# Memory projections without their 1/rms, and the rotary angles placed beside the FFN's down projection

## The chip, the core and the metric

The kernel runs on one core of a Trainium2 chip. The metric is the device time of one execution in microseconds (us); the time before is the median of three runs.

## The reference, cut to what matters

Two transformer blocks run one after the other on 256 tokens of 1024 features, all in fp32. The first block has two layers (a gated linear attention with FFN over context and tokens, then a latent attention, MLA, with FFN). The second block has one layer with three mixers; one of these attends to a memory of 256 rows, another uses a partial rotary embedding at given positions:

```python
kvm = rms_norm(mem, mem_norm_g) @ w_mem_kv            # 256 rows, 512 columns
km, vm = jnp.split(kvm, 2, axis=-1)
km = rms_norm(km.reshape(B, N_MEM, MEM_HEADS, HEAD_DIM), mk_norm_g)
...
ang = positions.astype(jnp.float32)[..., None] * inv_freq
cos = jnp.cos(ang)[:, :, None, :]
sin = jnp.sin(ang)[:, :, None, :]
```

The memory and the positions are inputs, so both pieces can be computed at any place ahead of the second block. `rms_norm(mem, g)` is mem * (1/rms of the row) * g. The factor 1/rms belongs to a row of the memory, so it can be applied after the product with the weights as well as before it.

## The kernel before, in words

Activations lie feature-major: 8 tiles of 128 features by 256 tokens. Each fp32 product is made of fp32r matmuls on split operands, hi and lo (`mm3`, lines 336 to 346): three matmuls of 256 columns, or one of 512 and one of 256 where hi and lo of the moving side lie together. Every weight travels the same road in one fixed list (`items`): a transfer by SP's queue into one of three `raw` buffers (line 275), a copy to hi on ScalarE (line 295), a subtraction to lo on VectorE (line 301) into one of four `wp` buffers. `weight()` asks for conversions three units ahead of the one that TensorE reads.

The order on each engine comes from the framework's scheduler. It takes program order as priority but puts an instruction forward when the engine would be free and its inputs are there, by its own estimate of durations. `tc.issue_after(x)` holds an instruction behind x on its engine.

The stages around the change, in program order:

- **MLA attention**, loop over `hd` from 0 to 9 (lines 1583 to 1592). Scores and softmax of head `hd`, transposes of head `hd-1`, values of head `hd-2`; steps 8 and 9 have only the ends of the last heads. In the same loop `mst.add` squares the memory tile by tile (ScalarE) and adds up (VectorE), which gives 1/rms of the memory's rows later. The query parts of head k lie in the half `MAIN` of the buffer `h`, feature tile k.
- **MLA output projection** (lines 1594 to 1600): 8 units of 8x3 matmuls. The first three units run together. After each unit `residual` (line 1146, VectorE) adds to `xT`, and `Stats.add` squares on ScalarE (line 538) and adds on VectorE (line 544, tile `sqa`). Woven into it are the steps of `normed_steps` for the memory: per feature tile a product with gain and 1/rms from PSUM (line 714, VectorE), a copy to hi (line 350, ScalarE) and a subtraction to lo (line 351, VectorE), into `h`'s half `MAIN`.
- **Memory key projection** (lines 1622 to 1624), 2 units of 24 matmuls. After the first 4 feature tiles (12 matmuls) the residual's statistics are closed (`st.rstd`: column sums by matmuls on line 518, a transpose on line 489, a square root on line 494, a reciprocal on line 496), then spread by two TensorE transposes (line 483), and `modulated` (lines 700 to 703) makes the input of the FFN. `m_evac` takes the keys from PSUM (line 1618) and squares them for the head norms.
- **Rotary angles** (lines 1632 to 1659): a small transfer of the positions by GpSimd's queue and 33 elementwise instructions of 128x256 on GpSimd; no other work is asked of GpSimd here.
- **FFN of the second layer**: 44 up units (22 steps of the loop over j, two units each), then a down projection of 8 outputs m with 4 weight units each (two of 6 and two of 5 feature tiles). `side()` is advanced once per j: sine and cosine at the seventh step, held behind a ScalarE instruction by `issue_after`, then the key norms.
- **End of the FFN**: the statistics of the new residual, `normed` for the second block, and the memory's value projection (lines 1691 to 1695).

`Stats` has a switch `ahead`: behind the square of the fourth tile it runs a dummy Sqrt (lines 499 to 505), so that the table for Sqrt is loaded before it is needed.

Of the kernel before, what the change touches and what calls it, by code (L numbers as in the profile page):

```python
# [10 lines left out]
F32 = mybir.dt.float32  # L11
F32R = mybir.dt.float32r
I32 = mybir.dt.int32
# [199 lines left out]
def body(tc, A, where, out, dbg=None):  # L213
# [48 lines left out]
    def width(i):  # L262
        us = items[i][1]
        return 2048 if us is None else sum(k * n for _, k, n in us)
# [6 lines left out]
    def top_up(n=NRAW):  # L271
        while at["dma"] < min(at["free"] + n, len(items)):
            j = at["dma"]
            r = wpool.tile([128, 2048], F32, tag="raw", name="raw", bufs=NRAW)
            SP.dma_start(r[:, :width(j)], items[j][0])
            raws[j] = r
            at["dma"] += 1

# [41 lines left out]
    class Two:  # L320


        def __init__(self, t):
            self.t = t
# [28 lines left out]
    def drain(g):  # L353
        for _ in g:
            pass
# [11 lines left out]
    def weave(main, fill, r=1):  # L367

        for _ in main:
            for _ in range(r):  # L370
                next(fill, None)
# [77 lines left out]
    def C(nm, grp="ca"):  # L449
        o, n = where[grp, nm]  # L450
        return ctile[grp][:, o:o + n]

    def vec(nm, i=0, n=1):
        o, _ = where[nm]
        return vecs[:, o + i:o + i + n]
# [50 lines left out]
    class Stats:  # L506

        def __init__(self, k, n, eng=None, halves=False, ahead=True):  # L510
            self.ahead = ahead and eng is not None
            self.k, self.n, self.c, self.sq, self.eng, self.mm = k, n, 0, None, eng, 0
            self.ns = None if halves else smbank()

# [14 lines left out]
        def add(self, t, square=True):  # L529
            self.flush()  # L530
            self.c += 1
            if not square:
                self.sq = t
                return
            n, inner = self.n, self.eng is not None and self.c < self.k
            head = inner and self.c == 1
            sq = tmp(512, "sqa" if head else "sq", 1 if head else 3)
            act = S.activation(sq[:, :n], t, AF.Square)
            if self.ahead and self.c == 4:
                table(AF.Sqrt, act)  # L540
            if head:
                self.acc = sq
            elif inner:
                self.eng.tensor_add(self.acc[:, :n], self.acc[:, :n], sq[:, :n])
            else:
                self.sq = sq
# [135 lines left out]
    def make_amp(layer, which, gname):  # L682

        need(layer, which * 3)
        need(layer, which * 3 + 1)
        for c in range(2):
            V.scalar_tensor_tensor(amp[:, layer, which, c, :], ada[layer][:, c, which * 24 + 8:which * 24 + 16],
                                   1.0, vec(gname, layer * 8, 8), op0=ALU.add, op1=ALU.mult)
# [19 lines left out]
    def normed_steps(src, gname, s, rr, dst, nb=None, ds=None, pool=()):  # L708
        nb = nb or spread(rr, 256)
        ds = ds or s  # L710
        hh, hl = dst[0], dst[1]
        for k in range(KT):
            u = tmp(512, "u", 2)
            V.scalar_tensor_tensor(u[:, :256], src[:, k, s], vec(gname, k), nb[:, :256], op0=ALU.mult, op1=ALU.mult)
            split_to(hh[:, k, ds], hl[:, k, ds], u[:, :256], G if k in pool else V)
            yield
# [857 lines left out]
    def mla_v(hd, PT):  # L1574
        po = mmbank()
        for kb in range(4):
            T.matmul(po[:, :256], vv[kb][:, hd * 128:(hd + 1) * 128], PT[:, kb, :], start=(kb == 0), stop=(kb == 3))  # L1577
        split_to(oh[0][:, hd, :256], oh[1][:, hd, :256], po[:, :256])

    memt = apool.tile([128, KT, 256], F32, name="memt")  # L1580
    G.dma_start(memt, A["memT"])
    mst = Stats(KT, 256, V, ahead=False)
    for hd in range(10):
        if hd >= 2:
            mst.add(memt[:, hd - 2, :])
        if hd < 8 and hd not in Pq:
            Pq[hd] = mla_s(hd)
        if 0 <= hd - 1 < 8:
            PTq[hd - 1] = mla_t(hd - 1, Pq.pop(hd - 1))
        if 0 <= hd - 2 < 8:  # L1590
            mla_v(hd - 2, PTq.pop(hd - 2))
    make_amp(1, 1, "norm_ffn")
    st = Stats(KT, 256, V)
    f = proj(both(I_mo), oh, HALF, lambda ps, m: residual(ps, m, 1, 2, (1,), st))
    next(f)
    mrr = mst.rstd(1024)
    weave(f, normed_steps(memt, "mem_g", HALF, mrr, h, None, MAIN))
    drain(f)
    mp.close()
    if dbg is not None and "x1a" in dbg:  # L1600
# [11 lines left out]
    kraw = lpool.tile([128, 2, 256], F32, name="kraw")  # L1612
    mhd = []

    def m_evac(ps, m):
        if m == 0:
            mhd.append(Heads(2, 256, 64, True))
        S.activation(kraw[:, m, :], ps, AF.Copy, scale=vec("mkg"))
        mhd[0].add(ps)


    f = proj(both([I_mem[0]]), h, MAIN, m_evac, 0)
# [3 lines left out]
    next(f)  # L1626
    modulated(1, 1, 1, spread(rr, 256), h, HALF)
    drain(f)

    ep_ = ExitStack()  # L1630
    epool = phase["pool"] = ep_.enter_context(tc.tile_pool(name="epool", bufs=1))
    post = tmp(256, "post", 1, I32)
    G.dma_start(post, A["pos"])


    ang = tmp(256, "ang", 1)
    G.tensor_copy(ang, post)
    G.tensor_scalar(ang, ang, C("invf", "cl"), None, op0=ALU.mult)
    twopi = Fraction("6.28318530717958647692528676655900576839433879875021164194988918461563")

    def fpieces(x, bits, n):
# [5 lines left out]
            yield float(v)  # L1647
            r -= v

    MAGIC = 12582912.0  # L1650
    kk, kv_ = tmp(256, "angk", 1), tmp(256, "angv", 1)
    for period, bits, n in ((twopi * 4096, 7, 8), (twopi, 11, 4)):
        G.tensor_scalar(kk, ang, float(1 / period), None, op0=ALU.mult)
        G.tensor_scalar(kk, kk, MAGIC, None, op0=ALU.add)
        G.tensor_scalar(kk, kk, MAGIC, None, op0=ALU.subtract)
        for v in fpieces(period, bits, n):
            G.tensor_scalar(kv_, kk, -v, None, op0=ALU.mult)
            G.tensor_add(ang, ang, kv_)
    G.tensor_scalar(ang, ang, math.pi, -math.pi, op0=ALU.min, op1=ALU.max)
    def side():  # L1660
        for _ in range(6):
            yield
        with tc.issue_after(mark["act"].ins):
            S.activation(sin2, ang, AF.Sin)
            S.activation(kk, ang, AF.Sin, scale=0.5)
        G.tensor_mul(kk, kk, kk)
        G.tensor_scalar(cos2, kk, -2.0, 1.0, op0=ALU.mult, op1=ALU.add)

        yield
        mhd[0].rstd()  # L1670
        yield
        for m in range(2):
            V.tensor_mul(km[:, m, :], kraw[:, m, :], mhd[0].spread(m))
            yield

    st = []

    def resid1(ps, m, last):
        if m == 0:
            st.append(Stats(KT, 256, V))  # L1680
        residual(ps[:, 256:], m, 1, 5, (1,), None)
        residual(ps[:, :256], m, 1, 5, (1,), st[0])

    ffn(1, h, (1,), False, resid1, side(), s=HALF)
    if dbg is not None and "x1b" in dbg:
# [6 lines left out]
    for t in range(2):  # L1692
        ps = mmbank()
        gemm_t(ps[:, :256], ws, h, 2 + t)
        S.activation(vm[:, t, :], ps[:, :256], AF.Copy)
    ep_.close()
    l2 = phase["pool"] = lp.enter_context(tc.tile_pool(name="l2pool", bufs=1))
    lcnt = C("lcnt", "cl").rearrange("p (t k) -> p t k", t=2)
# [261 lines left out]
```

## Time and profile before

| | us |
|---|---|
| runs (three) | 1309.72, 1310.82, 1315.43 |
| median | 1310.82 |
| the profiled execution, its time | 1309.43 |
| its span in the profile | 1307.7 |
| TensorE busy | 1265.2 (97%) |
| VectorE busy | 1076.0 (82%) |
| ScalarE busy | 748.3 (57%) |
| GpSimd busy | 84.8 (6%) |

The profile is one execution; times in it count from the start of its span. A row of a time line gives start, duration, engine, line, operation, output and inputs, and in brackets how long the engine sat idle before it and who released it. Matmuls overlap, so two of them started 0.12 us apart can each show 0.28 us. The engines are PE (TensorE; PEld its weight loads), DVE (VectorE), ACT (ScalarE), POOL (GpSimd) and SPq (SyncE's DMA queue).

### The profile page before, as it was taken

To read this page: it belongs to the slowest core of one execution; us is meant where nothing else is said; L and a number is where in the kernel's file an instruction comes from. 1 tells how busy PE (TensorE), PEld (TensorE's weight loads), DVE (VectorE), ACT (ScalarE), POOL (GpSimd) and SP (SyncE) were. 2 spreads that over 40 slices of the span, in tenths; PEclk is the share of its full clock that TensorE was granted. 3 is DMA by queue.
4 is the path that set the end of the run, shared out by engine and by line. 5 is a ranking of instruction groups with operands and counts; after the bars stand their busy time and mean duration, and the time that the engine had idled before them with its cause. 6 is when DMAs were issued, how large, how long until landed. Compare 5 with 4: busy or idle time off the path is not lost.

```text
span 1307.7 us, 20138 instructions
## 1 busy us (share of the span) xinstructions
PE 1265.2 (97%) x7612; PEld 1082.2 (83%) x7612; DVE 1076.0 (82%) x2261; ACT 748.3 (57%) x1324; POOL 84.8 (6%) x99
## 2 busy tenths in 40 slices
PE   6899999999999999999999998999999899999998
PEld 3779888898888888878987797888889777888887
DVE  3597987779999899879757878999757986899964
ACT  4686354444442244433476755887656777777742
POOL 0000000000000000000002046000000630000000
PEclk9999999999999999999999998999999899999999
DMA  9542344325445654446323113555555321455453
GB/s 375 194 163 95 134 170 148 129 92 188 172 163 195 228 185 179 141 140 217 134 81 129 65 47 130 197 190 184 170 196 180 142 98 65 162 195 200 175 192 109
DMA packets 32497, 207.55 MB, mean 159 GB/s; under 512 B 3760, under 2 KB 5040, under 8 KB 12176
## 3 DMA queue, kind: packets, MB, share of 16 engines
q1 hardware_dynamic: 31968, 204.17, 43.8%
q0 software_dynamic: 432, 2.10, 0.5%
q8 instruction: 60, 0.98, 0.3%
q14 instruction: 37, 0.30, 0.1%
HBM read 205.20 MB, written 1.05 MB: 158 GB/s over the span
## 4 chain that ended last, share of the span: by engine, by line
PE 82%; DVE 9%; ACT 4%; DMA 2%; issue 2%; POOL 1%; SPq 0%; POOLq 0%; DVEq 0%; ACTq 0%
PE mm L345 18%; PE mm L341 16%; PE mm L343 15%; PE mm L342 15%; PE mm L346 9%; DVE wp L301 2%; DMA a<-in_ada_dram 1%; DVE u L654 1%; ACT wp L295 1%; PE mm L1577 1%; DMA raw<-in_w_ada_dram 1%; PE sm L1024 1%; PE mm L1837 1%; PE sm L634 1%; PE mm L1046 1%
## 5 line engine op out<-in xcount | busy, mean ns | idle before, releaser
L301 DVE TENSOR_TENSOR wp<-raw,wp 128x1024 fp32r<-128x1024 f32 (+2 forms) x314 | 350.5, 1118 | 63.8 <-ACT wp L295 63.0
L295 ACT ACTIVATE wp<-raw 128x1024 fp32r<-128x1024 f32 (+2 forms) x316 | 305.0, 970 | 168.5 <-PE mm L343 87.8
L341 PE MATMUL mm<-hp,wp 128*128 128x512 f32 (+1 forms) x1004 | 346.4, 346 | 2.3 <-ACT hp L350 1.7
L342 PE MATMUL mm<-hp,wp 128*128 128x512 f32 (+1 forms) x1004 | 342.5, 342 | 3.1 <-DVE wp L301 3.1
L343 PE MATMUL mm<-hp,wp 128*128 128x512 f32 (+1 forms) x1004 | 338.8, 341 | 0.9 <-DVE hp L703 0.9
L345 PE MATMUL mm<-hp,wp 128*128 128x512 f32 x664 | 231.3, 394 | 0.6 <-DVE hp L351 0.5
L654 DVE SCALAR_TENSOR_TENSOR u<-raw,cb 128x512 f32<-128x512 f32 x320 | 204.8, 686 | 30.3 <-DMA raw<-in_w_ada_dram 25.3
L341 PEld LDWEIGHTS mm<-hp,wp 128*128 128x128 f32 x1004 | 191.6, 191 | 30.2 <-issue 5.7
L342 PEld LDWEIGHTS mm<-hp,wp 128*128 128x128 f32 x1004 | 192.1, 191 | 24.7 <-DVE wp L301 3.5
L343 PEld LDWEIGHTS mm<-hp,wp 128*128 128x128 f32 x1004 | 190.8, 191 | 22.7 <-DVE hp L703 1.6
L346 PE MATMUL mm<-hp,wp 128*128 128x256 f32 x664 | 184.4, 278 | 0.6 <-DVE wp L301 0.6
L345 PEld LDWEIGHTS mm<-hp,wp 128*128 128x128 f32 x664 | 124.4, 187 | 29.8 <-DVE hp L351 0.9
L346 PEld LDWEIGHTS mm<-hp,wp 128*128 128x128 f32 x664 | 125.0, 188 | 1.5 <-DVE wp L301 0.9
L345 PE MATMUL mm<-ap,wp 128*128 128x512 f32 x352 | 122.1, 392 | 0.0
L346 PE MATMUL mm<-ap,wp 128*128 128x256 f32 x352 | 98.4, 279 | 0.0
L1193 ACT ACTIVATE cv<-mm,vecs 128x512 f32<-128x512 f32 (+1 forms) x47 | 35.5, 765 | 78.5 <-PE mm L343 75.4
L345 PEld LDWEIGHTS mm<-ap,wp 128*128 128x128 f32 x352 | 66.0, 188 | 14.6
L343 PE MATMUL mm<-ap,wp 128*128 128x512 f32 (+1 forms) x198 | 72.5, 366 | 0.7 <-DVE ap L351 0.7
L341 PE MATMUL mm<-ap,wp 128*128 128x512 f32 (+1 forms) x198 | 72.7, 367 | 0.4 <-ACT ap L350 0.4
L342 PE MATMUL mm<-ap,wp 128*128 128x512 f32 (+1 forms) x198 | 72.4, 366 | 0.0
L346 PEld LDWEIGHTS mm<-ap,wp 128*128 128x128 f32 x352 | 66.3, 188 | 0.0
L341 PE MATMUL mm<-wp,hp 128*128 128x256 f32 (+1 forms) x192 | 58.4, 304 | 0.1
(327 smaller groups left out, 1893.9 us busy)
## 6 DMA issues: line engine op xcount, KB each, us to landing
raw<-in_up_dram SPq DMA_DIRECT2D x66, 1024.0 KB, 4.8
raw<-in_w_ada_dram SPq DMA_DIRECT2D x40, 1024.0 KB, 4.9
raw<-in_dn_dram SPq DMA_DIRECT2D x48, 704.0 KB, 4.0
raw<-in_gla_in_dram SPq DMA_DIRECT2D x12, 1024.0 KB, 5.6
raw<-in_in_dram SPq DMA_DIRECT2D x9, 1024.0 KB, 4.7
a<-in_ada_dram SPq DMA_DIRECT2D x8, 1024.0 KB, 19.5
raw<-in_gla_out_dram SPq DMA_DIRECT2D x4, 1024.0 KB, 5.8
raw<-in_mla_out_dram SPq DMA_DIRECT2D x4, 1024.0 KB, 4.7
```

Of the source, the lines that this page charges most:

```text
L295: S.activation(hi, r, AF.Copy)
L301: V.tensor_sub(w[:, 1, :kt * c], r, hi)
L341: T.matmul(ps, lhs[0], rhs[0], start=first, stop=False)
L342: T.matmul(ps, lhs[1], rhs[0], start=False, stop=False)
L343: T.matmul(ps, lhs[0], rhs[1], start=False, stop=last)
L345: T.matmul(ps.rearrange("p (a t) -> p a t", a=2), lhs[0], rhs[2], start=first, stop=False)
L346: T.matmul(ps[:, 256:], lhs[1], rhs[0], start=False, stop=last)
L634: T.matmul(nb, lhs, self.hl[j], start=(j == 0), stop=(j == 1))
L654: V.scalar_tensor_tensor(tmp(512, "u", 2), raws[n][:, ks], 1.0, cb[:, c, hf * 512:hf * 512 + 512], op0=ALU.mult, op1=ALU.mult, accum_out=p ...
L1024: T.matmul(pk[:, q * 256:(q + 1) * 256], kt_[:, q * 128:(q + 1) * 128], vv[:, t, q * 256:(q + 1) * 256], start=True, stop=True)
L1046: T.matmul(o, sm[:, q, v * 128:(v + 1) * 128], ep[:, d * 2 + q, blk(t)], start=False, stop=(n == len(use) - 1))
L1193: mark["act"] = S.activation(t[:, :n], ps, AF.Identity, bias=vec(cb, j), scale=vec(cw, 44 + j))
```

## The change

The memory goes into its projections as mem * gain, without 1/rms. The eight hi and lo steps for it (one ScalarE and one VectorE instruction each) move into steps 8 and 9 of the attention loop; the weave with `normed_steps` goes. The factor 1/rms is kept as a tile `mnb` (all partitions, one column per row of the memory) and as a column `mcol` (two TensorE transposes). Keys are multiplied with `mnb` as they leave PSUM, values get `mcol` as the scale of their copy. The angles become a function that `side()` calls at the 21st of 22 steps; the positions now come by SP's queue, behind the newest weight transfer; sine and cosine are taken behind the residual of m = 5 in the down projection, without `issue_after`; `ahead` becomes a number, and the Sqrt table of that stage comes behind the seventh square instead of the fourth.

```diff
@@ top_up
-            SP.dma_start(r[:, :width(j)], items[j][0])
+            mark["raw"] = SP.dma_start(r[:, :width(j)], items[j][0])
@@ Stats.add
-            if self.ahead and self.c == 4:
+            if self.c == self.ahead:
                 table(AF.Sqrt, act)
@@ the attention loop
             mla_v(hd - 2, PTq.pop(hd - 2))
+        if hd >= 8:
+            for k in range(4 * hd - 32, 4 * hd - 28):
+                g = vec("mem_g", k)
+                S.activation(h[0][:, k, MAIN], memt[:, k, :], AF.Copy, scale=g)
+                V.scalar_tensor_tensor(h[1][:, k, MAIN], memt[:, k, :], g, h[0][:, k, MAIN],
+                                       op0=ALU.mult, op1=ALU.subtract)
@@ the MLA output projection
     next(f)
     mrr = mst.rstd(1024)
-    weave(f, normed_steps(memt, "mem_g", HALF, mrr, h, None, MAIN))
     drain(f)
@@ the memory's key projection
+    mnb = lpool.tile([128, 256], F32, name="mnb")
+    S.activation(mnb, spread(mrr, 256)[:, :256], AF.Copy)
+    mcol = lpool.tile([128, 2], F32, name="mcol")
     def m_evac(ps, m):
         if m == 0:
             mhd.append(Heads(2, 256, 64, True))
-        S.activation(kraw[:, m, :], ps, AF.Copy, scale=vec("mkg"))
-        mhd[0].add(ps)
+        u = tmp(512, "u", 2)[:, :256]
+        V.tensor_mul(u, ps, mnb)
+        S.activation(kraw[:, m, :], u, AF.Copy, scale=vec("mkg"))
+        mhd[0].add(u)
...
     drain(f)
+    pt = smbank()
+    for t in range(2):
+        T.transpose(pt[:, t * 128:t * 128 + 128], mnb[:, t * 128:t * 128 + 128], ident)
+    S.activation(mcol, pt[:, 0:256:128], AF.Copy)
@@ the angles: the same GpSimd instructions, now in a function
+    def angles():
+        post = tmp(256, "post", 1, I32)
+        with tc.issue_after(mark["raw"].ins):
+            SP.dma_start(post, A["pos"])
...
+        return ang, kk
     def side():
-        for _ in range(6):
-            yield
-        with tc.issue_after(mark["act"].ins):
-            S.activation(sin2, ang, AF.Sin)
-            S.activation(kk, ang, AF.Sin, scale=0.5)
-        G.tensor_mul(kk, kk, kk)
-        G.tensor_scalar(cos2, kk, -2.0, 1.0, op0=ALU.mult, op1=ALU.add)
-        yield
         mhd[0].rstd()
         yield
         for m in range(2):
             V.tensor_mul(km[:, m, :], kraw[:, m, :], mhd[0].spread(m))
             yield
+        for _ in range(17):
+            yield
+        rot.extend(angles())
+        yield
@@ the FFN's residual
-            st.append(Stats(KT, 256, V))
+            st.append(Stats(KT, 256, V, ahead=7))
         residual(ps[:, 256:], m, 1, 5, (1,), None)
         residual(ps[:, :256], m, 1, 5, (1,), st[0])
+        if m == 5:
+            ang, kk = rot
+            S.activation(sin2, ang, AF.Sin)
+            S.activation(kk, ang, AF.Sin, scale=0.5)
+            G.tensor_mul(kk, kk, kk)
+            G.tensor_scalar(cos2, kk, -2.0, 1.0, op0=ALU.mult, op1=ALU.add)
@@ the memory's value projection
-        S.activation(vm[:, t, :], ps[:, :256], AF.Copy)
+        S.activation(vm[:, t, :], ps[:, :256], AF.Copy, scale=mcol[:, t:t + 1])
```

## Rows read from the trace of the kernel before

**Rows 1.** The page's chain that ended last, shares of the span by engine.
```profile
PE 82%; DVE 9%; ACT 4%; DMA 2%; issue 2%; POOL 1%; SPq 0%; POOLq 0%; DVEq 0%; ACTq 0%
```

**Rows 2.** Windows: start:end, length, busy of PE, PEld, DVE, ACT, POOL, clock, DMA.
```profile
747.00:752.00 5.00, 5.00 (x28) 4.32 (x27) 3.51 (x8) 2.58 (x8) 0.00 (x0) 1.00 0.00 0
...
786.00:791.50 5.50, 5.50 (x48) 5.50 (x47) 5.50 (x10) 3.22 (x7) 5.08 (x5) 1.00 0.42 170
791.50:795.70 4.20, 0.25 (x3) 0.05 (x2) 4.20 (x7) 1.62 (x3) 3.94 (x4) 0.88 0.66 250
...
798.00:801.40 3.40, 3.40 (x21) 3.35 (x16) 0.80 (x3) 1.90 (x4) 3.06 (x5) 0.50 0.85 306
```

**Rows 3.** Time line of PE around the end of the MLA output projection.
```profile
771.33 0.38 PE L483 MATMUL sm<-ca,rr 128*128 128x128 f32 x2
...
791.47 0.28 PE L343 MATMUL mm<-hp,wp 128*128 128x256 f32 x1
795.72 0.44 PE L518 MATMUL sm<-sqa,ones 128*32 128x64 f32 x8 [3.98 <-DVE sqa L544]
...
799.07 0.41 PE L342 MATMUL mm<-hp,wp 128*128 128x256 f32 x1
799.28 0.41 PE L343 MATMUL mm<-hp,wp 128*128 128x256 f32 x1
```

**Rows 4.** PE groups, 766.1 to 791.55: line, operation, tiles, shape, count, busy, mean ns.
```profile
L341 PE MATMUL mm<-hp,wp 128*128 128x256 f32 x68 | 19.5, 287 | 0.0
```

**Rows 5.** DVE groups by form, 771 to 796: busy us, mean ns, idle before.
```profile
L301 DVE TENSOR_TENSOR wp<-raw,wp 128x1024 fp32r<-128x1024 f32 x8 | 10.8, 1345 | 0.0
L351 DVE TENSOR_TENSOR hp<-u,hp 128x256 fp32r<-128x256 f32 x8 | 5.2, 656 | 0.1
L544 DVE TENSOR_TENSOR sqa<-sqa,sq 128x256 f32<-128x256 f32 x6 | 4.4, 727 | 0.0
L714 DVE SCALAR_TENSOR_TENSOR u<-memt,vecs,sm 128x256 f32<-128x256 f32 x8 | 3.7, 476 | 2.0 <-PE sm L483 1.9
```

**Rows 6.** DVE groups by form, 810 to 920 (the FFN's up projection).
```profile
L301 DVE TENSOR_TENSOR wp<-raw,wp 128x1024 fp32r<-128x1024 f32 x40 | 48.7, 1218 | 0.8 <-ACT wp L295 0.4
...
L351 DVE TENSOR_TENSOR ap<-cv,ap 128x256 fp32r<-128x256 f32 x19 | 7.9, 417 | 0.1
```

**Rows 7.** DVE groups by form, 930 to 985 (the FFN's down projection).
```profile
L544 DVE TENSOR_TENSOR sqa<-sqa,sq 128x256 f32<-128x256 f32 x6 | 2.5, 419 | 0.0
```

**Rows 8.** Time line of DVE where the FFN ends and the second block begins.
```profile
990.58 0.48 DVE L1146 SCALAR_TENSOR_TENSOR xT<-mm,ada,xT 128x256 f32<-128x256 f32 x1
...
992.25 0.25 DVE L489 STREAM_TRANSPOSE rs<-sm 128x64 f32<-128x64 f32 x1
...
993.82 0.87 DVE L714 SCALAR_TENSOR_TENSOR u<-xT,vecs,sm 128x256 f32<-128x256 f32 x2 [0.79 <-PE sm L483]
```

**Rows 9.** Windows late in the up projection and inside the down projection.
```profile
912.00:920.00 8.00, 8.00 (x49) 7.06 (x48) 7.84 (x16) 6.23 (x12) 0.00 (x0) 1.00 0.34 115
...
940.00:960.00 20.00, 20.00 (x117) 17.76 (x116) 12.06 (x20) 9.51 (x13) 0.00 (x0) 1.00 0.58 199
```

**Rows 10.** Time line of ACT: first sine, last Silu of the FFN, load for Sqrt.
```profile
849.97 0.40 ACT L1664 ACTIVATE sin<-ang 128x256 f32<-128x256 f32 x1
...
931.55 0.42 ACT L1226 ACTIVATE cv<-cv 128x256 f32<-128x256 f32 x1
...
960.54 1.28 ACT L504 ACT_TABLE_LOAD   x1
```

**Rows 11.** Issue on SP's queue of the third transfer of down-projection weights.
```profile
920.32 0.33 SPq L275 DMA_DIRECT2D raw<-in_dn_dram  x1
```

**Rows 12.** POOL groups by form, 767 to 808: the two largest of the angles.
```profile
L1658 POOL TENSOR_TENSOR ang<-ang,angv 128x256 f32<-128x256 f32 x12 | 13.0, 1086 | 1.0
L1657 POOL TENSOR_SCALAR angv<-angk 128x256 f32<-128x256 f32 x12 | 11.4, 953 | 1.0
```

**Rows 13.** Waits of ACT for POOL, second block: total us, times, longest.
```profile
ACT cvp L1731 <- POOL cacp L1732: 1.7, 4, 0.8
```

More of the change, by code (lines that the diff above doesn't have):

```diff
@@ L506, in body, with __init__ @@
     class Stats:
-        def __init__(self, k, n, eng=None, halves=False, ahead=True):
-            self.ahead = ahead and eng is not None
+        def __init__(self, k, n, eng=None, halves=False, ahead=4):
+            self.ahead = ahead if eng is not None else 0
             self.k, self.n, self.c, self.sq, self.eng, self.mm = k, n, 0, None, eng, 0
@@ L1581, in body @@
     G.dma_start(memt, A["memT"])
-    mst = Stats(KT, 256, V, ahead=False)
+    mst = Stats(KT, 256, V, ahead=0)
     for hd in range(10):
@@ L1628, in body @@
     drain(f)
+    pt = smbank()
+    for t in range(2):
+        T.transpose(pt[:, t * 128:t * 128 + 128], mnb[:, t * 128:t * 128 + 128], ident)
+    S.activation(mcol, pt[:, 0:256:128], AF.Copy)
     ep_ = ExitStack()
     epool = phase["pool"] = ep_.enter_context(tc.tile_pool(name="epool", bufs=1))
[L1632 to L1638, printed above, removed]
     twopi = Fraction("6.28318530717958647692528676655900576839433879875021164194988918461563")
@@ L1648, in fpieces @@
             r -= v
[L1650 to L1659, printed above, removed]
-    def side():
-        for _ in range(6):
-            yield
-        with tc.issue_after(mark["act"].ins):
-            S.activation(sin2, ang, AF.Sin)
-            S.activation(kk, ang, AF.Sin, scale=0.5)
-        G.tensor_mul(kk, kk, kk)
-        G.tensor_scalar(cos2, kk, -2.0, 1.0, op0=ALU.mult, op1=ALU.add)
-        yield
+    def angles():
+        post = tmp(256, "post", 1, I32)
+        with tc.issue_after(mark["raw"].ins):
+            SP.dma_start(post, A["pos"])
+        ang = tmp(256, "ang", 1)
+        G.tensor_copy(ang, post)
+        G.tensor_scalar(ang, ang, C("invf", "cl"), None, op0=ALU.mult)
+        MAGIC = 12582912.0
+        kk, kv_ = tmp(256, "angk", 1), tmp(256, "angv", 1)
+        for period, bits, n in ((twopi * 4096, 7, 8), (twopi, 11, 4)):
+            G.tensor_scalar(kk, ang, float(1 / period), None, op0=ALU.mult)
+            G.tensor_scalar(kk, kk, MAGIC, None, op0=ALU.add)
+            G.tensor_scalar(kk, kk, MAGIC, None, op0=ALU.subtract)
+            for v in fpieces(period, bits, n):
+                G.tensor_scalar(kv_, kk, -v, None, op0=ALU.mult)
+                G.tensor_add(ang, ang, kv_)
+        G.tensor_scalar(ang, ang, math.pi, -math.pi, op0=ALU.min, op1=ALU.max)
+        return ang, kk
+    def side():
         mhd[0].rstd()
@@ L1674, in side @@
             yield
+        for _ in range(17):
+            yield
+        rot.extend(angles())
+        yield
+    rot = []
     st = []
```

## The prediction, made before the change was run

> **What bounds the kernel now.** I read the chain of waits first: TensorE holds 82% of it and VectorE 9% [rows 1]. So a step is worth something only where TensorE waits for it. Next come the windows around the edited lines. In the attention TensorE is busy throughout at full clock, VectorE 3.51 us of 5 and ScalarE 2.58 [rows 2]. Late in the MLA output projection VectorE is busy without a gap, 5.50 of 5.50, with GpSimd beside it at 5.08; then TensorE falls to 0.25 of 4.20 us, and from 798 to 801.4 its granted clock is 0.50 [rows 2]. The reader should see one place: VectorE late, TensorE idle, then TensorE at its lower level, 1.2 instead of 2.4 GHz.
>
> The time line of TensorE names the wait: the last matmul starts at 791.47, and the column sum at 795.72 sat idle 3.98 us for the running sum of squares on VectorE [rows 3]. Afterwards two matmuls start 0.21 us apart [rows 3]. Up to the stop there were 3 x 68 = 204 of them in some 25.4 us, 0.12 us each [rows 4], so TensorE had no gap before it: 192 are the output projection, 12 the first quarter of the memory's keys. The projection itself therefore ends 12 x 0.12 = 1.4 us earlier, at about 790.1.
>
> Why VectorE is late: between 771 and 796 it makes 10.8 us of weight conversions, 5.2 us of lo parts of the memory, 3.7 us of products with gain and 1/rms, and 4.4 us of running sums [rows 5]. Three of these groups are slower than where GpSimd rests: the conversion takes 1345 ns against 1218 [rows 5, 6], the lo part 656 against 417 for the same operation and shape [rows 5, 6], the running sum 727 against 419 [rows 5, 7]. The product that reads PSUM shows no such spread: 476 ns beside GpSimd [rows 5]. So GpSimd's angles cost VectorE 8 x 0.13 + 8 x 0.24 + 6 x 0.31 = 4.8 us in this stretch.
>
> **What the change removes.** VectorE loses from the stretch 3.7 us of products and 5.2 us of lo parts [rows 5], and of the 4.8 us of GpSimd's slowing the 2.9 that fell on what stays. That is 11.8 us of work out of a stretch of 24 in which it had no gap. It fell 795.72 - 791.55 = 4.2 us behind TensorE; with 11.8 us less it is no longer behind, and the running sum is ready before TensorE asks.
>
> So the wait of 3.98 us goes [rows 3]. The stretch at the lower clock behind it goes too, since it follows the only stop of TensorE here: from 795.72 to about 801.4, 5.7 us at 0.21 us a matmul instead of 0.12, of which 5.7 x (1 - 0.12/0.21) = 2.4 us are lost [rows 3, 4]. Together -6.4 us. From 801.4 on TensorE is fed, so nothing more can be gained here.
>
> **What is late next.** The last residual still has to pass square, column sum, transpose, root, spread. The same chain stands at the end of the FFN, where GpSimd rests: residual at 990.58, transpose at 992.25, first product of the next stage at 993.82 [rows 8], 3.2 us, and about 1 us more for its hi and lo. In the new kernel the residual starts near 790.3, so the FFN's first input is there near 794.6. TensorE meanwhile has 48 matmuls of keys, 5.8 us from 790.1, column sums and spread aside: until about 796. The cover is 1.3 us longer than the chain. The key products with `mnb` are two VectorE instructions more, near 0.42 us each by the two-input rows [rows 6]. The first stands ahead of the FFN's modulation and the second inside it; queued behind are the modulated tiles, and TensorE waits for those. The 1.3 us of cover hide both, so 0; without the cover, 0.8.
>
> **What it adds.** (1) Two transposes for `mcol`: a pair shows 0.38 us on TensorE [rows 3], and no other engine hides TensorE's own time. +0.4. (2) Eight ScalarE copies and eight VectorE instructions in the attention. They are independent of the heads still running once head k's scores are done, so the scheduler may put them into any idle gap from there, not only the two last steps. VectorE has 1.5 us free in five, ScalarE 2.4 [rows 2]: the room is there. But a softmax step can queue behind one. Bounds: 0 if they all fall in gaps, and 8 x 0.2 = 1.6 us if each costs a head half of a 0.42 us instruction. A gain is excluded, since TensorE has no gap there. Nearer to the row is the low end, as VectorE is 30% idle: +0.3. (3) Positions by SP's queue: one short transfer behind the newest weights. The weight transfers of the down projection use 0.58 of the DMA engines [rows 9]; it passes between them, 0. If the queue had no room it would hold a weight by less than its own length, hidden by three units of weights ahead. (4) The Sqrt load of 1.28 us [rows 10] moves from the fourth to the seventh square, still beside a down projection in which ScalarE is busy 9.51 of 20 [rows 9]: 0. Sine, cosine, their two GpSimd products and the scale on the values' copy lie there too or replace like by like: 0.
>
> (5) **The angles beside the FFN.** They are asked for at step 21 of 22, behind the third transfer of down-projection weights, which now issues at 920.32 [rows 11] and then about 6 us earlier. Two groups of twelve took 24.4 us beside a full VectorE [rows 12]; the whole chain of 33 at that rate is some 34 us. So its first 6 to 8 us lie beside the end of the up projection, where VectorE is busy 7.84 of 8 [rows 9], and the rest beside the down projection, 12.06 of 20 [rows 9]. By the trace VectorE loses 4.8 in 24, about 0.2 us per us, so 1.2 to 1.6 us there; weights are converted three units of some 2.8 us ahead, which hides it: 0. Bounds 0 and 1.6; a gain is excluded, since TensorE is busy 8.00 of 8 there [rows 9].
>
> The Trainium skill, "SBUF — State Buffer", section on the two sides of SBUF, says that VectorE with two SBUF inputs and GpSimd lock one shared port pair, and that the loser is blocked for the whole instruction. By that rule each VectorE instruction of this kind beside the angles could lose up to one GpSimd instruction, and this change would move the stop rather than remove it. The rows agree in which instructions slow down, and show 0.13 to 0.31 us each, not a whole GpSimd instruction of 0.95 to 1.09.
>
> **The sum.** -6.4 + 0.4 + 0.3 = -5.7 us, against the profiled execution's 1309.4: 1303.7. The median of the runs is 1310.8, 1.4 above that execution, so I forecast 1305.1. About 0.5%, 6.6 us, is what a measurement of this kernel can tell from no change; the border is 1304.3.
>
> **Rivals.**
> *A, the forecast.* Own range 1303 to 1307, 0.66. Runs before scatter by over 1 us to below, and with both additions at nothing the sum is -6.4, so a good part lies past the border: 0.30 of this 0.66.
>
> *B, the stop comes back as a wait for the modulated input.* The keys' inputs are now ready long before their turn. If the scheduler uses their 48 matmuls as filler inside the output projection, TensorE has nothing left when that ends and idles for the chain of 4.3 us, minus little, and again drops to the lower clock: +4 to +6, 1309 to 1311. For it: the scheduler did put 12 of them ahead of the column sum. Against it: up to 791.5 TensorE has no gap to fill [rows 4]. 0.12.
>
> *C, the angles' collision.* If VectorE loses more beside GpSimd than [rows 5 to 7] show, the end of the up projection is where it hurts, since VectorE is 98% busy there [rows 9]. Six to eight GpSimd instructions of about 1 us [rows 12], each holding back a VectorE instruction, make 6 to 8 us, of which the weights ahead hide about 5: +1 to +3, 1306 to 1308. This is the rule of "SBUF — State Buffer" at its full price. 0.10.
>
> *D, slower: the sine stops ScalarE.* Nothing holds the sine behind a given instruction any more. If the scheduler takes GpSimd's chain for shorter than it is, it puts the sine early, as far forward as the last Silu, at 931.55 in the old time line [rows 10], some 925 in the new. ScalarE then waits for the angles until about 917 + 34 = 951, and behind it queue all weight conversions. Three units of down-projection weights ahead carry TensorE some 5.7 us; of 26 us, 20 are left, and 2.4 for the clock: 1305.1 + 22.4 = 1327.5. It decides from a lateness of 5.7 us on, and turns into a slowdown past the border from about 15. Against it: where the second block hands ScalarE's products to GpSimd, ScalarE waited only 1.7 us in four waits [rows 13], so GpSimd's durations are not far misjudged; and at its own place, behind m = 5, the sine is some 15 us later than the angles. 0.12, of which 0.10 past the border.
>
> **How the numbers follow.** Faster: 0.30, from A. Slower: 0.10, from D. The rest is 0.60: what is left of A, B, C and the mild end of D. The range takes in A, B and C, 0.88, with half a us below A for scatter: 1302.5 to 1311.5.
>
> **What would show it.** In the profile after: no wait of the column sum on line 518 over 0.5 us, clock 1.00 through the output projection and the keys, GpSimd idle between 770 and 806, running sums back near 420 ns there, and the FFN's first matmul about 6 us earlier with nothing given back until the second block. B would show as an idle of TensorE in front of the FFN's first matmuls, C as conversions near 1.4 us and a wait of TensorE late in the up projection, D as a wait of ScalarE for GpSimd at the sine. The forecast is wrong if the stop stays although VectorE is free there: then the wait was not VectorE's load but the chain itself.

## The result, and the profile after

The changed kernel takes 1330.47 us (median of 4 runs, 1326.89 to 1333.78), the kernel before 1310.49 us (4 runs, 1309.72 to 1315.43). The ratio is 1.0143, with a 95% interval of 1.0119 to 1.0166: slower by about 19 us. The forecast of 1305.1 us, with a range up to 1311.5, was wrong. It came out as rival D had it, which the prediction put at 1327.5 us and gave 0.12.

In the chain that ended last, by engine, GpSimd has 3% where [rows 1] had 1%, at VectorE's expense:

```profile
PE 83%; DVE 6%; ACT 5%; POOL 3%; DMA 2%; issue 2%; SPq 0%; POOLq 0%; ACTq 0%; DVEq 0%
```

TensorE's waits from 780 on show the place (engine, line, what it waited for; us in total, times, longest):

```profile
PE mm L345 <- ACT wp L295: 15.2, 1, 15.2
PE sm L1851 <- DVE P L1526: 4.6, 3, 2.0
PE sm L634 <- issue: 3.9, 1, 3.9
PE mm L346 <- DVE wp L301: 1.5, 2, 0.9
```

The wait of the column sum in front of the FFN (line 518, [rows 3]) is gone from the list. In its place TensorE waits 15.2 us, once, inside the down projection, for a weight conversion by ScalarE. The time line of ScalarE says why that conversion was late:

```profile
930.44 0.42 ACT L350 ACTIVATE ap<-cv 128x256 fp32r<-128x256 f32 x1 [0.61 <-DVE cv L1227]
931.20 0.85 ACT L295 ACTIVATE wp<-raw 128x768 fp32r<-128x768 f32 x1 [0.34 <-PE mm L346]
952.74 0.42 ACT L1703 ACTIVATE sin<-ang 128x256 f32<-128x256 f32 x1 [20.69 <-POOL ang L1678]
953.06 0.40 ACT L1704 ACTIVATE angk<-ang 128x256 f32<-128x256 f32 x1
953.37 0.72 ACT L295 ACTIVATE wp<-raw 128x640 fp32r<-128x640 f32 x1
```

The sine on line 1703 stands right behind a weight conversion that ended at 932.05. ScalarE takes its instructions in order, so it waited there 20.69 us for the angles, and the next conversion of weights came only at 953.37. The angles were still being made. These are the first, two middle and the last of their 33 instructions in the time line of GpSimd, 921.53 to 952.71:

```profile
921.53 0.69 POOL L1667 CAST ang<-post 128x256 f32<-128x256 int32 x1 [153.52 <-DVE wp L301]
...
947.08 0.85 POOL L1676 TENSOR_SCALAR angv<-angk 128x256 f32<-128x256 f32 x1
948.01 0.72 POOL L1677 TENSOR_TENSOR ang<-ang,angv 128x256 f32<-128x256 f32 x1
...
952.31 0.40 POOL L1678 TENSOR_SCALAR ang<-ang 128x256 f32<-128x256 f32 x1
```

The windows around the stop (start:end, length, busy of PE, PEld, DVE, ACT, POOL, clock) show everything but GpSimd at rest (TensorE's 3.94 us lie ahead of the stop), and TensorE at its lower level, 1.2 GHz, behind the stop:

```profile
935.00:951.00 16.00, 3.94 (x23) 3.16 (x21) 0.00 (x0) 0.00 (x0) 14.47 (x19) 0.74 0.00 1
951.00:957.00 6.00, 2.80 (x7) 2.09 (x8) 2.66 (x4) 3.75 (x7) 3.12 (x5) 0.50 0.17 32
957.00:965.00 8.00, 8.00 (x40) 6.88 (x39) 4.55 (x7) 2.77 (x5) 0.00 (x0) 0.82 0.68 246
```

The place that the prediction was about did what it said. The same stretches as in [rows 2], after the change:

```profile
786.00:791.50 5.50, 5.50 (x52) 5.37 (x54) 3.90 (x7) 3.00 (x5) 0.00 (x0) 1.00 0.56 195
791.50:795.70 4.20, 4.20 (x49) 4.11 (x50) 2.92 (x6) 2.46 (x5) 0.00 (x0) 1.00 0.58 185
798.00:801.40 3.40, 3.40 (x22) 2.48 (x21) 3.22 (x7) 1.43 (x5) 0.00 (x0) 1.00 0.40 118
```

TensorE is busy through all of them at full clock, GpSimd is silent, and VectorE has room. Its operations are quick again where [rows 5] had 1345 and 727 ns (groups by form, 771 to 796):

```profile
L301 DVE TENSOR_TENSOR wp<-raw,wp 128x1024 fp32r<-128x1024 f32 x9 | 10.9, 1220 | 2.2 <-ACT wp L295 2.2
L544 DVE TENSOR_TENSOR sqa<-sqa,sq 128x256 f32<-128x256 f32 x6 | 2.5, 420 | 0.1
```

**Where the 17.4 us between the two spans lie** (1325.1 less 1307.7). A common base is needed, since executions differ already ahead of the edited lines: I take the first matmul of line 1566, at 731.8 before and 731.2 after. From there to the first down matmul it is 196.5 us before and 193.8 after, -2.7. The down projection, first matmul to last, takes 79.7 instead of 60.9, +18.8. From there to the end of the span it is 320.4 instead of 318.5, +1.9. With the -0.6 of the base that is 17.4. So 5.3 us were won in front of the FFN (its first column group ends at 807.16 instead of 813.1, less the base's 0.6), 2.6 of them were given back in the up projection, and the down projection cost 18.8.

### The profile page after: what moved, and what is told of

Read it like the earlier page. It is cut to its first block, busy times and chain, and to the rows that moved or that the text cites. A ratio compares the mean times of both kernels' runs of the same rounds, so it can differ in the third digit from the quotient of the medians.

```text
span 1325.1 us, 20142 instructions
## 1 busy us (share of the span) xinstructions
PE 1269.9 (96%) x7614; PEld 1083.5 (82%) x7614; DVE 1070.1 (81%) x2255; ACT 746.0 (56%) x1324; POOL 77.7 (6%) x98
## 4 chain that ended last, share of the span: by engine, by line
PE 83%; DVE 6%; ACT 5%; POOL 3%; DMA 2%; issue 2%; SPq 0%; POOLq 0%; ACTq 0%; DVEq 0%
PE mm L341 16%; PE mm L345 16%; PE mm L342 16%; PE mm L343 16%; PE mm L346 8%; DVE wp L301 2%; DMA a<-in_ada_dram 1%; ACT wp L295 1%; PE mm L1577 1%; POOL angv L1676 1%; PE sm L1024 1%; PE mm L1046 1%; POOL ang L1677 1%; PE mm L1861 1%; DVE u L654 1%
## 5 line engine op out<-in xcount | busy, mean ns | idle before, releaser
L342 PEld LDWEIGHTS mm<-hp,wp 128*128 128x128 f32 x1004 | 191.9, 191 | 24.6 <-DVE wp L301 3.5
L345 PE MATMUL mm<-ap,wp 128*128 128x512 f32 x352 | 125.1, 399 | 15.2 <-ACT wp L295 15.2
L345 PEld LDWEIGHTS mm<-ap,wp 128*128 128x128 f32 x352 | 67.3, 191 | 31.2 <-ACT wp L295 15.5
## 6 DMA issues: line engine op xcount, KB each, us to landing
a<-in_ada_dram SPq DMA_DIRECT2D x8, 1024.0 KB, 18.8
```

The lines of the kernel that those rows point to most:

```text
L342: T.matmul(ps, lhs[1], rhs[0], start=False, stop=False)
L345: T.matmul(ps.rearrange("p (a t) -> p a t", a=2), lhs[0], rhs[2], start=first, stop=False)
```

## The experiments

The kernels came in three groups, each against runs of the kernel before on the same chip. The table gives, of each profiled execution, the way from the first matmul of line 1566 to the first down matmul ("to down"), the down projection and the rest to the end of the span, in us.

| kernel | ratio to before, 95% | to down | down | rest |
|---|---|---|---|---|
| before | 1 | 196.5 | 60.9 | 318.5 |
| changed | 1.0143 (1.0119 to 1.0166) | 193.8 | 79.7 | 320.4 |
| e1, changed, sine held | 0.9995 (0.998 to 1.0009) | 193.8 | 62.1 | 320.4 |
| e2, memory's part alone | 1.0004 (0.9985 to 1.0022) | 192.5 | 62.1 | 323.8 |
| e3, angles' part alone | 1.0107 (1.0088 to 1.0126) | 191.5 | 78.1 | 323.7 |
| e4, changed, shorter chain | 1.0048 (1.0032 to 1.0065) | 193.8 | 71.3 | 318.9 |
| e5, e12, angles' part, sine held | 0.9953 (0.9937 to 0.9969), 0.9958 (0.9943 to 0.9974) | 191.9, 191.9 | 60.9, 61.5 | 321.8, 318.7 |
| e6, e1 with the key norm put back | 0.9978 (0.9964 to 0.9992) | 192.1 | 62.1 | 321.9 |
| e11, e5 with the key norm put back | 0.9928 (0.991 to 0.9947) | 190.5 | 60.9 | 319.0 |
| e7, before again | one execution, 1313.51 us | 196.5 | 60.9 | 320.5 |
| e8, e1 again | one execution, 1319.08 us | 193.8 | 62.1 | 322.0 |
| e9, e1, held behind block 1 | one execution, 1322.74 us | 195.5 | 71.8 | 322.1 |
| e10, e1, held behind block 2 | one execution, 1311.48 us | 193.9 | 63.4 | 322.2 |

Single profiles scatter too: the rest is 2.0 us longer in e7 than in the first profile of the same kernel, 1.6 in e8 than in e1. And in e3 and e9 "to down" begins with 3.4 us at a granted clock of 0.50 (from 734.5 and 734.2), 1.7 us lost that no other profile has there.

**The sine held back (e1).** In the changed kernel, with the square of the residual remembered at each output block:

```diff
-            S.activation(sin2, ang, AF.Sin)
-            S.activation(kk, ang, AF.Sin, scale=0.5)
+            with tc.issue_after(mark["sq"].ins):
+                S.activation(sin2, ang, AF.Sin)
+                S.activation(kk, ang, AF.Sin, scale=0.5)
```

> The changed kernel, with the sine held behind the square of the residual of m = 5 on ScalarE. Theory Q (queue): the scheduler put the sine where it believed GpSimd's chain to end, some 20 us too early, and the weight conversions queued behind it. Then the wait of ScalarE for GpSimd and the 15.2 us wait of TensorE are gone, the down projection takes 61 us as before instead of 79.7, and what is left is the hand-over won ahead of the FFN: 1305 to 1309. Theory P (port): GpSimd beside the down projection slows the conversions on VectorE by their shared port; then the place of the sine does not matter and the time stays at 1325 to 1331. Theory M (memory part): the new steps of the memory cost more than they save; then it stays over 1313.

Measured: 1310.33 us against 1311.25, a little over the 1305 to 1309 expected. The sine moved behind the square of block 5, where the angles had long been there (time line of ScalarE):

```profile
972.94 0.42 ACT L538 ACTIVATE sq<-xT 128x256 f32<-128x256 f32 x1 [0.32 <-DVE xT L1146]
973.27 0.40 ACT L1704 ACTIVATE sin<-ang 128x256 f32<-128x256 f32 x1
973.57 0.40 ACT L1705 ACTIVATE angk<-ang 128x256 f32<-128x256 f32 x1
```

It waits for nothing, TensorE's 15.2 us are gone, and the down projection takes 62.1 us. Nothing was changed but the place of two instructions in ScalarE's order, so that place is the cause of the loss, some 19 us (1.0143 against 0.9995). GpSimd's angles lie beside the down projection as before, so contention of VectorE and GpSimd is not the cause.

**One part alone (e2, e3).** e2 has the memory's projections without 1/rms, and the angles in their old place; e3 has the angles beside the down projection, and the memory as before; its sine has no hold. Cut to their core, e2 against the changed kernel and e3 against the kernel before:

```diff
     def side():
-        mhd[0].rstd()
...
-        rot.extend(angles())
+        for _ in range(6):
+            yield
+        with tc.issue_after(mark["act"].ins):
+            S.activation(sin2, ang, AF.Sin)
...
```

```diff
-    ang = tmp(256, "ang", 1)
-    G.tensor_copy(ang, post)
...
+    def angles():
+        post = tmp(256, "post", 1, I32)
+        with tc.issue_after(mark["raw"].ins):
+            SP.dma_start(post, A["pos"])
...
+        rot.extend(angles())
```

> Only the memory's part of the change; angles, sine, key norm and positions as before. If VectorE's own work (8.9 us less in the stretch that was 4.2 us late) was the cause of the stop in front of the FFN, the stop of 3.98 us goes though GpSimd still works beside it: 1303 to 1308. If the slowing by GpSimd was the cause, the stop stays for the most part: 1309 to 1312. Theory M: over 1313.

> Only the angles' part of the change (function called at step 21, positions by SP's queue, sine behind m = 5 without a hold); the memory as before. Theory Q: the sine waits about 20 us on ScalarE, TensorE 15 us for a conversion; before + 19 in the down projection, less up to 6 if the stop in front of the FFN goes with GpSimd's slowing: 1323 to 1331. Theory M: the loss lies in the other part, so 1304 to 1312 here.

Measured: 1312.04 and 1325.55 us against 1311.25; e2 missed the 1303 to 1308 that its expectation drew from the stop going. The loss belongs to the angles' part; waits in e3, 915 to 1000:

```profile
ACT sin L1686 <- POOL ang L1661: 19.6, 1, 19.6
PE mm L345 <- ACT wp L295: 13.8, 1, 13.8
```

And the stop in front of the FFN is gone in each of the two. Column sums in the time line of TensorE, e2:

```profile
795.42 0.32 PE L518 MATMUL sm<-sqa,ones 128*32 128x64 f32 x8
795.99 0.32 PE L518 MATMUL sm<-sq,ones 128*32 128x64 f32 x8 [0.25 <-ACT sq L538]
```

and e3:

```profile
793.32 0.32 PE L518 MATMUL sm<-sqa,ones 128*32 128x64 f32 x8
794.48 0.32 PE L518 MATMUL sm<-sq,ones 128*32 128x64 f32 x8
```

The prediction's working had said as much without drawing the conclusion: VectorE was 4.2 us late, the memory's part takes 8.9 us from it and the angles' part 4.8 (its total of slowing), so each by itself is enough. Once the angles are elsewhere, the memory's part has no stop left to remove. In e2's profile the way to the down projection is 4.0 us shorter, and what follows is 6.5 us longer (1.2 and 5.3). The slower of two paces (below), which it has in both FFNs, accounts for 1.2 and 3.3 of that. It is one profile of an execution of 1315.38 us; why the median of the 12 runs (1305.55 to 1317.22) is no better than before, it doesn't show.

**A shorter chain (e4).** The changed kernel without the first of the two range reductions of the angles, 14 GpSimd instructions instead of 33; what is left out is that reduction.

```diff
-        for period, bits, n in ((twopi * 4096, 7, 8), (twopi, 11, 4)):
+        for period, bits, n in ((twopi, 11, 4),):
```

> The changed kernel with the first of the two passes of range reduction left out: 14 GpSimd instructions in the chain instead of 33 (the second pass alone still brings the angles into range). Theory Q, with an error that grows with every GpSimd instruction: the sine's wait falls from 20.7 to about 20.7 x 14/33 = 8.8 us, TensorE's from 15.2 to about 3.3, the time to 1308 to 1315. Rival T: the chain is judged rightly, but its start (the transfer of the positions) is late by a constant; then sine and chain both move forward, the wait stays near 20 us and the time at 1325 to 1331.

Measured: 1317.39 us against 1311.25, over the 1308 to 1315 expected. Waits, 915 to 1000:

```profile
ACT sin L1703 <- POOL ang L1678: 8.5, 1, 8.5
PE mm L345 <- DVE ap L351: 6.8, 1, 6.8
```

ScalarE's wait shrank with the chain: 8.5 us for 14 instructions, 20.7 for 33, 19.6 for 33 in e3, which is 0.61, 0.63 and 0.59 us an instruction. The sine stands where a chain of about 0.3 us an instruction would end: 4.2 us behind the chain's start in e4 (925.43 less 921.19), 10.5 in the changed kernel (932.05 less 921.53). On the chip an instruction took 31.2 / 33 = 0.95 us. So the order was made with a third of GpSimd's real duration, which the rows fit but which was not read from the planner itself. TensorE's wait was larger than the theory gave for this run, since the sine had moved forward as well, among ScalarE's last instructions of the up projection: what TensorE lacked was the input of the down projection, not a weight, and less of that was in store: 8.5 less 6.8 is 1.7 us.

**The hold moved forward (e9, e10).** e1 with the sine held behind the square of block 1 or 2, to measure what the weight units ahead cover:

```diff
-        if m == 5:
+        if m == 1:
```

> The changed kernel with the two sine instructions held behind the square of the residual's output block 1 instead of 5. The computation is whole. In the first profile with the hold that square began at 941.85, and GpSimd's angles end at about 952.3. Theory (ScalarE waits for the angles at the sine, the conversions behind it wait with it, and the weight units ahead cover about 5.5 us, 20.7 less 15.2 in the changed kernel): ScalarE waits about 10 us at the sine, TensorE 4 to 5.5 us for a conversion some 5 us later, down projection 66.5 to 69 us, span 1312 to 1316. Rival (a sine anywhere inside the down projection costs TensorE a fixed 7 to 15 us, as the two places measured so far did): TensorE waits over 6.5 us. Rival (any hold is enough, it is the order against the other engines that counts): no wait of TensorE over 1 us.

> The same with the sine held behind the square of output block 2, which began at 949.62 in the first profile with the hold. The computation is whole. Theory (the units ahead cover 5.5 us): ScalarE waits 2 to 3 us for the angles at the sine, TensorE not at all (under 0.5 us), down projection 62.0 to 62.6 us at the pace of 0.353 us, or 61 at 0.347; span within 2 us of 1307.5. Rival (no cover, what ScalarE waits TensorE waits): TensorE waits 2 us or more, down projection 64 us or more.

Measured, waits from 915 to 1000 in e9:

```profile
ACT sin L1704 <- POOL ang L1678: 11.4, 1, 11.4
PE mm L345 <- ACT wp L295: 6.6, 1, 6.6
```

and in e10:

```profile
ACT sin L1704 <- POOL ang L1678: 5.1, 1, 5.1
PE mm L346 <- DVE wp L301: 0.5, 1, 0.5
PE mm L345 <- ACT wp L295: 0.4, 1, 0.4
```

ScalarE's waits of 20.7, 11.4 and 5.1 us became 15.2, 6.6 and 0.9 us of TensorE. The cover is 5.5, 4.8 and 4.2 us, not a fixed loss and not none. e9 is a miss by size: TensorE was to wait 4 to 5.5 us and the down projection to take 66.5 to 69, and it was 6.6 and 71.8, since the angles ended at 955.7, 3.4 later than in the execution that I had read, and the lower clock behind the stop cost 3 us more. Its 6.6 us alone would also fit the rival of a fixed loss (over 6.5); e10 rules that one out. e10 waited a little longer than expected too (5.1 instead of 2 to 3), TensorE 0.9 instead of under 0.5, and its down projection took 63.4 us instead of 62.0 to 62.6.

**Why e1 gains nothing (e5, e6, e11, e12).** e1 had won its 5 us in front of the FFN and was still no faster than before. e5 and e12 are one kernel, e3 with the hold of e1. e6 and e11 let the first step of the key norm wait for the seventh step of the up projection's loop, one step ahead of its place before the change:

```diff
     def side():
+        for _ in range(6):
+            yield
         mhd[0].rstd()
...
-        for _ in range(17):
+        for _ in range(11):
```

> The kernel before with the angles' part of the change alone (GpSimd computes them beside the down projection) and with the two sine instructions held behind the square of the residual's output block 5, so that ScalarE meets them late. The computation is whole. Theory (the loss was the place of the sine in ScalarE's order, and nothing else of the angles costs): no wait of ScalarE for the angles over 1 us, no wait of TensorE inside the down projection over 1 us, down projection 61 to 62.2 us, and the stop of 4.0 us before the column sum gone as in the angles' part without the hold, so the first down matmul at 923 to 924.5 and the second block 2 us longer than before (its wait for P 2.2 instead of 1.0 and the clock's fall behind it); sum about -3, less or more by the pace of the 512-column matmul: ratio 0.995 to 1.000. Rival (the angles on GpSimd themselves slow the other engines): as in e1_guard or worse, down projection 63 us or more, ratio 1.001 or more. Rival (the memory's part is what gave the gain of the hand-over back in e1_guard, by 2.5 us in the up projection): 2.5 us under e1_guard, ratio 0.9975 or less.

> The same kernel as e5_angles_guard (the kernel before with the angles' part alone and the sine held), timed again. Theory (the gain of 0.47% is the kernel's): ratio 0.9935 to 0.997, no overlap with 1. Rival (it was the luck of one call): ratio 0.998 or more.

> The changed kernel with the sine held as in e1_guard, and the first step of the key norm put back by six calls, to where it stood before the change, so that its statistics don't stand ahead of the first weight conversions of the FFN. The computation is whole. Theory (the gain of 5.9 us in front of the FFN was given back in three places: a wait of 0.9 us for the first conversions behind the key norm, the slower of two paces of the 512-column matmul, and the wait for P in the second block): the wait of L346 for the conversion by VectorE, 0.9 us, is gone, the first down matmul comes 0.9 to 1.5 us earlier than e1_guard's 925.0 at the same pace, all else as in e1_guard; ratio 0.9975 to 1.000. Rival (the key norm's place is worth nothing: what is cheap there is dear later): the first down matmul within 0.4 us of 925.0, or a new wait of 0.5 us or more near the seventh call, ratio 0.999 to 1.001.

> The kernel before with the angles' part alone, the sine held behind block 5, and the key norm put back to the seventh call. The computation is whole. Theory (the key norm's place is worth something only where the memory's part puts more work of ScalarE in front of the FFN: without that part no wait of 0.9 us for a conversion showed): the first down matmul within 1 us of 923.8, ratio within 0.002 of e5's (0.993 to 0.997). Rival (the key norm ahead of the first conversions costs 2 to 3 us by itself, as between the two versions of the whole change): first down matmul at 920.5 to 922, ratio 0.991 to 0.994.

Measured: e5 0.9953 and e12 0.9958, e6 0.9978, e11 0.9928. The angles' part with the hold is faster than before, and that was no luck of one measurement. e5 is also faster than e1, by more than their intervals, as its rival on the memory's part had it (0.9975 or less). With the key norm put back like this the first down matmul comes 1.7 us earlier in the whole change (193.8 to 192.1) and 1.4 in the angles' part alone (191.9 to 190.5). In e6 the wait of 0.9 us of line 346 is gone, and the eight column sums of the key norm (line 591) take 1.1 us of TensorE's time instead of 1.7; the pace (below) is the slower one in both e1 and e6. For e11 I had expected nothing, because e5 shows no wait of 0.9 us for a conversion. The forecast missed, but no wait explains it: e11's matmul pairs run at the faster pace from 842 on, where two matmuls of the key norm stand between them, and e5's only from the first down matmul on. That is some 220 pairs at 6.6 ns, 1.5 us, all of the 1.4. So only e6 shows a worth of the key norm's place by itself. e11 has the lowest ratio here, 0.7% under the kernel before (1303.78 us against 1313.21). Its stretch beside the angles has TensorE busy throughout:

```profile
925.00:955.00 30.00, 30.00 (x175) 26.57 (x174) 22.69 (x30) 14.31 (x21) 26.74 (x26) 1.00 0.55 188
```

**Two paces of the same matmul pair (e7, e8).** The kernel before, and e1, each profiled once more without an edit.

> The kernel before, unchanged, profiled once more. In its first profile the pair of 512- and 256-column matmuls (L345 and L346) came every 0.347 us in the up and the down projection of both FFNs; in the changed kernels' profiles it is 0.347 or 0.353, one value from a stall to the next. Theory (the pace is settled by the execution, at each stall anew): at least one of the four projections shows the other pace, 0.353 us, here or in one of the next profiles of an unchanged kernel, and the time follows at 1.1 to 2.3 us a projection. Rival (the pace belongs to the program): 0.347 in all four again, span within 1 us of 1307.7 less what other stages differ.

> The same kernel as e1_guard (the changed kernel with the sine held), profiled once more. Its first profile has a pace of 0.353 us in the up and down projection of the first FFN and 0.347 in the second. Theory (the pace is the execution's): another pattern, with 328 pairs in the up and 176 in the down projection at 6.6 ns each, so the first down matmul up to 2.2 us earlier (922.8) and the down projection 62.1 or 60.9 us. Rival (the program's): 0.353, 0.353, 0.347, 0.347 again and the first down matmul at 925.0 within 0.5 us.

The pairs of lines 345 and 346 run at one of two paces, without any wait: starts 0.347 or 0.353 us apart. It shows in the mean of the 512-column matmul in 20 us of the down projection (950 to 970). The kernel before, second profile:

```profile
L345 PE MATMUL mm<-ap,wp 128*128 128x512 f32 x59 | 20.5, 390 | 0.0
```

and e1:

```profile
L345 PE MATMUL mm<-ap,wp 128*128 128x512 f32 x58 | 20.5, 396 | 0.0
```

Over the 176 pairs of a down projection that is 62.1 less 60.9 us, over the 328 of an up projection about 2. In the first FFN, e7 and e8 repeat the pattern of their first profiles (0.347 and 0.353, each from 826 on at the latest), and so do their ways to the down projection, 196.5 and 193.8 us. In the second FFN e5 and e12, one kernel, differ: 0.353 and 0.347, which is the 3 us between their rests of 321.8 and 318.7. So neither theory holds alone: in three repeats of three the first FFN kept its pace, and the one change of pace without a change of code is in the second. In the first FFN's down projection the pace even goes with the code: all six profiles without the memory's part have 0.347, all eight with it 0.353, but for the changed kernel behind its stop (a mean of 0.349). That is a pattern; what sets the pace stays open.

For e1's sum this gives: to the down projection it has -2.7 us where 5.3 were won: 0.9 are the wait for the first conversions, which now stand behind the key norm, and 1.7 to 2 are the slower pace in the up projection. The down projection loses 1.2 by the pace. The rest is 1.9 longer, with 4.7 us of TensorE's waits for `P` by VectorE in the second block instead of 3.6. That is not the change's doing: in e7, which has none of it, the rest is 2.0 longer, and the same wait is as long (e7, from 780 on):

```profile
PE sm L1827 <- DVE P L1526: 4.6, 3, 2.1
```

The granted clock from 985 to 1130 is 0.98 in all three profiles. Together +0.4 on the base, and -0.6 ahead of it: the span of 1307.5 against 1307.7.

## Why the prediction was wrong, step by step

- **The stop goes, with its stretch at the lower clock (-6.4), transposes and attention (+0.7): right.** Forecast -5.7 at the FFN's first matmuls, measured -5.3 on the common base. VectorE's slowing by GpSimd left as the rows had said: 1345 to 1220 ns and 727 to 420.
- **"Nothing given back until the second block": wrong, and small.** Of 5.3 us, 0.9 went to a wait that the moved key norm opened, which the prediction had not costed at all, and 1.7 to a slower pace that no row of before shows.
- **"Sine, cosine ... lie there too: 0", and the sine "at its own place, behind m = 5, is some 15 us later than the angles": the step that failed.** The place in the source is not the place in the engine's order. With its hold taken away, the sine was put 10.5 us behind the chain's start, and the chain took 31.2. e1 shows that this alone is the loss.
- **The evidence against rival D was no evidence.** That ScalarE waited only 1.7 us for GpSimd in the second block [rows 13] was read as "GpSimd's durations are not far misjudged". Those waits are of short steps, alternating between two engines, in which each wait was 0.8 us at most; a chain of 33 adds up its error 33 times. The chain's real length was in the rows (24 instructions in 24.4 us, [rows 12]); what the planner takes it for was in none, and the chance had to stay open for that.
- **Rival D was priced well.** A wait of ScalarE of 26 us was forecast and 20.7 measured; a cover of 5.7 and 5.5; TensorE's wait 20 and 15.2; 2.4 us for the clock and some 3.1 measured (79.7 less 60.9 less 15.2, with half a us of pace in it). Its total was 1327.5 us against 1330.47, and its sign in the profile, a wait of ScalarE for GpSimd at the sine, is the first line to read. Only its chance was wrong. That the total came within 3 us is luck in part: the stop with its clock was priced 3.6 us too dear, and the 5.7 us gained in front, which D kept whole, shrank to 2.7.
- **Angles beside the FFN cost TensorE nothing by contention: right, shown by e1 and e11.** VectorE is slowed there: in e1, 925 to 952, its running sum takes 958 ns, against 419 in [rows 7]. That is the mean of two; the six behind the 727 of [rows 5] are four of some 611 ns and two of 955 and 962, the same sizes in another mix. But VectorE has room, and no wait of TensorE follows. The Trainium skill, "SBUF — State Buffer", section on the two sides of SBUF, lets the loser of the shared port stand until the other's instruction is done. The 190 and 540 ns more per running sum, beside GpSimd instructions of 850, are less than a whole one. And as far as GpSimd's spans can be trusted the rule does not hold for every pair: of the eight lo parts of [rows 5], three lie inside a GpSimd instruction from start to end (at 773.57, 774.42 and 782.87) and took 410 to 418 ns, no longer than alone.
- **The memory's part by itself brings nothing measurable (e2), and next to the angles' part the kernel is slower with it.** The prediction had let the two reliefs add up against one lateness of 4.2 us. e11, without the memory's part, is 0.5% faster than e6 with it (0.9928 and 0.9978, intervals apart). By their profiles 1.6 us of that lie ahead of the down projection, 1.2 in it and 2.9 behind it. All three are of the pace's size (e6 has the slower one in both FFNs, e11 the faster from 842 on), so whether the part costs anything by its own work stays open.

## What to carry to other kernels

When a change takes away what held an instruction in place, ask where a planner will put it and what it believes of the engine that it waits for; on an engine that works in order, one instruction put too early stops everything behind it. A long chain on a slow engine is where such an error adds up: hold its consumer behind a late mark, here one line, worth some 1.5%. And when two parts of a change relieve the same stop, try each alone before keeping both.

## What the runs showed that was not expected

The two paces of the matmul pair, 0.347 and 0.353 us, are worth 3.3 us an FFN (504 pairs at 6.6 ns), as much as most edits here. They come without a wait in the profile and can change without one (e11 at 842; e5 and e12 at the first down matmul), and must be looked at before a difference of a quarter per cent is given to an edit. The gain of one stage can be lost to them in the next, as in e1.

The scatter between executions lies largely ahead of the edited lines: the first matmul of line 1566 comes at 731.2 us in e1 and at 739.4 in e8, the same kernel. A difference of two profiles says something only from a common base on, and behind the FFN not even then below some 2 us.
